# A decoder trunk's attention: how the first two groups load, keep and split their input blocks

## The chip, the core and the metric

The kernel runs on one core of one Trainium2 chip. A core has the engines TensorE (PE, matrix products), VectorE (DVE), ScalarE (ACT), GpSimd (POOL) and SyncE (SP, which here issues the DMA transfers), each with its own queue of instructions that it works through in order. The metric is the device time of one execution in microseconds (us), as the median of several.

## The reference

Two layers of a trunk over x of 1024 positions by 1024 channels, in float32. The first layer mixes by dilated sliding-window attention, the second by a gated recurrence, and after each comes a two-layer perceptron; every sub-layer ends in `x <- LayerNorm(alpha * x + sublayer(x))`. Cut to the part that the change is about:

```python
def dilated_attention_mixer(x, w_in, w_out):
    proj = (x @ w_in).reshape(B, S, N_GROUPS, 3, ATTN_HEADS, ATTN_HEAD_DIM)
    for g, (window, dilation) in enumerate(((128, 1), (512, 4), (2048, 16))):
        q, k = rotary(proj[:, :, g, 0], pos), rotary(proj[:, :, g, 1], pos)
        o, lse = dilated_window_attention(q, k, proj[:, :, g, 2], window, dilation)
    wts = softmax(stack(lses))
    return einsum('gbsh,gbshe->bshe', wts, stack(outs)) @ w_out
```

The second layer's recurrence also needs a few constants that depend on the weights alone (`forget_lower_bounds(lb_logits)`) and a causal mask.

## The kernel before

**Projections.** A unit is a pair of heads in one dilation. There are 24, taken two at a time: 12 groups. A group's q, k and v (j = 0, 1, 2: three pairs of weight blocks) are computed by the seven products of a Winograd-Strassen scheme, so a group is 21 products; product number n is 21 times the group, plus 3 times the place of the operand in `ORDA` = (2, 1, 6, 7, 4, 5, 3), plus j. The operand i is made of the transposed input's four blocks "11", "12", "21", "22" (`load_x`, two tiles of 128x1024 each): operands 1, 2 and 3 are the blocks "11", "21" and "22" themselves, 5, 6, 7 and 4 are the sums T1, T2, T3 and T4 (`combine_x`, on DVE). For float32 accuracy each operand, of x as of the weights, is split in a high half (a copy on ACT, line 131) and a low half (a subtraction on DVE, line 132), so a product is 12 matmuls of 128x512: xh by the weight's high half (line 644), xl by it (645), xh by the weight's low half (646).

**Where operands come from.** In group 0 `make_T` computes and splits each operand, and `keep_T` (line 371) spills the four tiles of its halves, 0.5 MB each, into the DRAM tensor xtd, one operand at each of the products in `KEEP`. In all later groups `get_T` (line 385) reads the halves back from xtd, the high half five products ahead and the low half three. Weights come by `load_w` (line 396, tiles wa and wb), are combined and split by `split_w_` (lines 409 to 417) and get their low half in `low_w` (line 425).

**What follows a product.** Its result (tile pmm in PSUM) is evicted by ACT (lines 667, 671) or added on DVE (669, 677, 679) into e, or vT for j = 2. A unit whose e are complete is rotated: `rope` moves e by four DMAs (line 453) into rot, POOL multiplies rot with the sine (455), DVE e with the cosine (456) and DVE adds the two (457) into qT or kT. Then come the scores s (line 483), the softmax (494, 497), the transposed probabilities (507, 510) and the output o (522). These steps of one group are placed between the products of the next, by the numbers in `ROPES` and `OFFS`. `constants` (line 432) loads cosine, sine, mask and the selector selw, which ACT copies to bsel (line 438), all at product 11. `hgrn_consts` (line 1353) computes the recurrent layer's constants by 29 small instructions on DVE and three on ACT, and loads its mask into cmf and casts it to cm; the program calls it after attention.

**Order.** A scheduler orders instructions on each engine by its own model, within the dependencies. The class `in_order` (line 101) adds dependencies so that an engine follows the order in which the program is written; in attention it holds for PE and DVE. ACT, POOL and SP are ordered by the scheduler, which also put most of `hgrn_consts` between the instructions of products 8 to 15. SP has eight semaphores for its transfers: from the ninth on an issue waits until the transfer eight places before has landed.

## Time and profile before

| | before |
|---|---|
| median of 3 runs | 2917.54 us (2911.75 to 2921.99) |
| the profiled execution | 2914.81 us, its span 2913.0 us |
| busy: PE, DVE, ACT, POOL | 2809.4, 2080.0, 1451.5, 430.4 us |
| mean granted TensorE clock | 0.986 of full speed |
| the DMA queue | 533.06 MB, 54.1% of the 16 engines' span |

The busy time of an engine is the sum of its instructions' durations; times in the rows below are counted from the start of the span. A start in brackets gives the idle time of the engine before that instruction and what ended it: `[2.26 <-DMA lg<-in_lb_logits_dram]` is 2.26 us of idleness that the landing of lg ended. The granted clock is the share of full speed that TensorE was given: 1.00 stands for 2.4 GHz, 0.50 for 1.2 GHz, and a stretch between them is a mixture.

### The profile page before, as it was taken

How to read it: one execution, taken by the hardware profiler on the slowest of the kernel's cores; microseconds unless marked ns; L12 is line 12 of the kernel's file. 1: busy time of each engine (PE TensorE's matmuls, PEld its weight loads, DVE VectorE, ACT ScalarE, POOL GpSimd, SP SyncE). 2: the span in 40 equal slices, each digit the busy share in tenths (PEclk: the TensorE clock that was granted, in tenths of full speed). 3: DMA queues.
4: the chain of work that ended last, by engine and by line, in shares of the span. 5: the costliest groups of instructions: out<-in, count | busy, mean ns of one | idle time of the engine just before them, and what ended most of it. 6: DMA issues, size and time to landing. Idle time of an engine off the chain costs nothing.

```text
span 2913.0 us, 40585 instructions
## 1 busy us (share of the span) xinstructions
PE 2809.4 (96%) x14152; PEld 2246.6 (77%) x14152; DVE 2080.0 (71%) x3717; ACT 1451.5 (50%) x3136; POOL 430.4 (15%) x211
## 2 busy tenths in 40 slices
PE   7899999999999999999999999999999999999998
PEld 6677777777777767788878886778787788878885
DVE  7678676777877668787677867555667787678776
ACT  5354555555455553644454535554553544454442
POOL 0112111111211102100061411101101200033300
PEclk9999999999999999999999999999999999999999
DMA  8876777678677533464484744101132465484653
GB/s 335 298 257 201 239 252 240 221 269 283 191 251 252 183 100 127 142 230 156 148 320 131 251 134 131 41 33 58 37 123 82 150 206 178 148 309 152 210 175 113
DMA packets 219325, 535.65 MB, mean 184 GB/s; under 512 B 32112, under 2 KB 46448, under 8 KB 219120
## 3 DMA queue, kind: packets, MB, share of 16 engines
q1 hardware_dynamic: 219120, 533.06, 54.1%
q8 instruction: 111, 1.82, 0.3%
q14 instruction: 94, 0.77, 0.1%
HBM read 408.96 MB, written 98.44 MB: 174 GB/s over the span
## 4 chain that ended last, share of the span: by engine, by line
PE 82%; DVE 7%; DMA 7%; issue 2%; ACT 1%; SPq 1%; POOL 0%; DVEq 0%; ACTq 0%; POOLq 0%
PE pup L1075 6%; PE pup L1073 6%; PE pup L1074 6%; PE pmm L645 6%; PE pmm L644 6%; PE pmm L646 6%; PE pdy L1214 4%; PE pdy L1213 4%; PE pdy L1210 4%; PE pmm L165 3%; PE pmm L166 3%; PE pmm L167 3%; PE pdx L1210 3%; PE pdx L1213 3%; PE pdx L1214 3%; PE s L483 2%
## 5 line engine op out<-in xcount | busy, mean ns | idle before, releaser
L644 PE MATMUL pmm<-xh,H 128*128 128x512 f32 x1008 | 411.0, 408 | 13.8 <-ACT H L417 8.0
L645 PE MATMUL pmm<-xl,H 128*128 128x512 f32 x1008 | 400.3, 397 | 14.3 <-DMA xl<-xtd 13.9
L646 PE MATMUL pmm<-xh,H 128*128 128x512 f32 x1008 | 399.4, 396 | 1.2 <-DVE H L425 1.2
L455 POOL TENSOR_TENSOR rot<-rot,sinT 128x1024 f32<-128x1024 f32 x48 | 141.7, 2956 | 858.9 <-DMA rot<-e 457.7
L644 PEld LDWEIGHTS pmm<-xh,H 128*128 128x128 f32 x1008 | 193.4, 192 | 54.8 <-ACT H L417 8.0
L645 PEld LDWEIGHTS pmm<-xl,H 128*128 128x128 f32 x1008 | 193.1, 192 | 54.5 <-DMA xl<-xtd 16.4
L646 PEld LDWEIGHTS pmm<-xh,H 128*128 128x128 f32 x1008 | 192.5, 191 | 43.8 <-DVE H L425 2.2
L494 DVE CUSTOM_DVE_ANT_0 p<-s,mask 128x128 f32<-128x128 f32 (+1 forms) x384 | 113.1, 348 | 139.8 <-PE s L483 129.8
L497 ACT ACTIVATE p<-p,stats 128x128 f32<-128x128 f32 (+1 forms) x384 | 168.2, 440 | 64.4 <-DVE stats L494 64.0
L1214 PE MATMUL pdy<-dT,dS 128*128 128x512 f32 x512 | 199.3, 389 | 0.0
L1213 PE MATMUL pdy<-dT,dS 128*128 128x512 f32 x512 | 199.3, 389 | 0.0
L1210 PE MATMUL pdy<-dT,dS 128*128 128x512 f32 x512 | 199.3, 389 | 0.0
L132 DVE TENSOR_TENSOR dS<-dr,dS 128x512 fp32r<-128x512 f32 x192 | 167.9, 874 | 22.8 <-ACT dS L131 22.4
L131 ACT ACTIVATE dS<-dr 128x512 fp32r<-128x512 f32 x192 | 119.9, 625 | 114.3 <-PE pdy L1214 57.5
L510 ACT ACTIVATE pts<-ppt 128x256 f32<-128x256 f32 (+1 forms) x192 | 85.6, 472 | 145.6 <-PE ppt L507 142.7
L165 PE MATMUL pmm<-f0nh,wh 128*128 128x512 f32 x384 | 153.3, 399 | 0.8 <-ACT wh L131 0.8
L167 PE MATMUL pmm<-f0nh,wl 128*128 128x512 f32 x384 | 150.0, 391 | 0.0
L166 PE MATMUL pmm<-f0nl,wh 128*128 128x512 f32 x384 | 149.9, 390 | 0.0
L1182 POOL TENSOR_TENSOR hold<-hold,dr 128x512 f32<-128x512 f32 x32 | 47.4, 1480 | 554.6 <-DVE upa L1115 517.5
L1034 ACT ACTIVATE H<-wc 128x512 fp32r<-128x512 f32 x128 | 77.2, 625 | 73.5 <-DVE wc L1027 44.2
L132 DVE TENSOR_TENSOR dT<-dr,dT 128x512 fp32r<-128x512 f32 x128 | 109.7, 862 | 4.2 <-ACT dT L131 3.5
L1213 PEld LDWEIGHTS pdy<-dT,dS 128*128 128x128 f32 x512 | 96.1, 188 | 20.1
(395 smaller groups left out, 7192.9 us busy)
## 6 DMA issues: line engine op xcount, KB each, us to landing
xh<-xtd SPq DMA_DIRECT2D x154, 512.0 KB
xl<-xtd SPq DMA_DIRECT2D x154, 512.0 KB
dr<-hd SPq DMA_DIRECT2D x192, 256.0 KB
dr<-in_w_down_dram SPq DMA_DIRECT2D x160, 256.0 KB
rot<-e SPq DMA_DIRECT2D x192, 128.0 KB
wa<-in_w_up_dram SPq DMA_DIRECT2D x48, 512.0 KB
wa<-in_w_attn_dram SPq DMA_DIRECT2D x36, 512.0 KB
wb<-in_w_attn_dram SPq DMA_DIRECT2D x36, 512.0 KB
```

The source lines that it names most:

```text
L132: nc.vector.tensor_sub(lo, raw, hi.bitcast(F32))
L165: nc.tensor.matmul(o, wh[:, k], xs.h(k), start=k == 0, stop=False)
L166: nc.tensor.matmul(o, wh[:, k], xs.l(k), start=False, stop=False)
L167: nc.tensor.matmul(o, wl[:, k], xs.h(k), start=False, stop=k == NK - 1)
L644: nc.tensor.matmul(o, wh, hi[k // 2][:, c], start=begin and k == 0, stop=False, skip_group_check=True)
L645: nc.tensor.matmul(o, wh, lo[k // 2][:, c], start=False, stop=False, skip_group_check=True)
L646: nc.tensor.matmul(o, wl, hi[k // 2][:, c], start=False, stop=end and k == 3, skip_group_check=True)
L1073: nc.tensor.matmul(o, wh, xf.h(b, k), start=begin and k == 0, stop=False, skip_group_check=True)
L1074: nc.tensor.matmul(o, wh, xf.l(b, k), start=False, stop=False, skip_group_check=True)
L1210: nc.tensor.matmul(o[q], h, T_[:, L], start=begin, stop=False, skip_group_check=True)
L1213: nc.tensor.matmul(o[q], h, T_[:, R], start=False, stop=False, skip_group_check=True)
L1214: nc.tensor.matmul(o[q], l, T_[:, L], start=False, stop=end, skip_group_check=True)
```

## The change

- 26 transposes of the identity, into a PSUM bank that nobody reads, stand ahead of all PE work.
- SP follows the written order up to the weights of the first eight products, in which the first weight now comes between the two halves of the first block of x; then SP and ACT follow it up to product 21.
- T1 and T2 are made one half after the other, and T2's split is postponed behind the work of products 2 and 3 (`soon`).
- The three operands that are plain blocks are not spilled in group 0. Group 1 reads the blocks of x again and splits them again, and spills them then. `KEEP` says at which product which operand is spilled.
- The selector's load, copy and a memset move from product 11 to product 36.
- `hgrn_consts` is called at product 40, inside the written order of DVE.

```diff
--- before.py
+++ after.py
@@ -47,7 +47,7 @@
 LOADW = 8
 SPLITW = 5
 UNIT0 = 3
-KEEP = (4,6,8,10,12,14,16)
+KEEP = {10: 2, 13: 3, 16: 4, 19: 5, 23: 7, 26: 8, 41: 13}
 MIX = (5, 6, 7, 10, 11, 12, 13, 14, 15)
 ROPES = ((-5, -2, -1, 2), (-4, 0, 1, 4))
 OFFS = ((0, 2, 4, 7, 9, 11), (10, 12, 15, 17, 19, 21))
@@ -313,7 +313,7 @@
         return t
 
 
-    def attention(pre):
+    def attention(pre, hc):
         cosT = U("cosT")
         sinT = U("sinT")
         units = [(pr, g) for pr in range(NPAIR) for g in GORD]
@@ -332,12 +332,17 @@
 
         xtd = dp.tile([7, 2, P, 2048], F32, name="xtd")
         opT, xr, xc = {}, {}, {}
-
-        def load_x(b):
+        soon = []
+
+
+        PLAIN = {1: "11", 2: "21", 3: "22"}
+
+        def load_x(b, between=lambda: None):
             half, k0 = int(b[1]) - 1, (int(b[0]) - 1) * 2048
             xr[b] = [U("x" + b) for _ in range(2)]
             for q in range(2):
                 nc.sync.dma_start(xr[b][q], xT[half, :, k0 + q * 1024:k0 + (q + 1) * 1024])
+                between()
 
         def combine_x(name, x, y, eng):
             xc[name] = [U("x" + name) for _ in range(2)]
@@ -347,13 +352,19 @@
         def make_T(i):
             v, g = nc.vector, nc.gpsimd
             if i == 6:
-                combine_x("T1", xr["12"], xr["11"], v)
-                combine_x("T2", xr["22"], xc["T1"], v)
+                for n_ in ("T1", "T2"):
+                    xc[n_] = [U("x" + n_) for _ in range(2)]
+                out_ = [U("xh", F32R) for _ in range(2)], [U("xl", F32R) for _ in range(2)]
+                for q in range(2):
+                    v.tensor_sub(xc["T1"][q], xr["12"][q], xr["11"][q])
+                    v.tensor_sub(xc["T2"][q], xr["22"][q], xc["T1"][q])
+                    soon.append(lambda q=q: split(xc["T2"][q], out_[0][q], out_[1][q]))
+                return out_
             elif i == 7:
                 combine_x("T3", xr["22"], xr["12"], v)
             elif i == 4:
                 combine_x("T4", xr["21"], xc["T2"], v)
-            src = {1: "11", 2: "21", 6: "T2", 7: "T3", 3: "22", 5: "T1", 4: "T4"}[i]
+            src = PLAIN.get(i) or {6: "T2", 7: "T3", 5: "T1", 4: "T4"}[i]
             src = xc.pop(src) if src == "T3" or src == "T4" else xc[src] if src in xc else xr[src]
             hi = [U("xh", F32R) for _ in range(2)]
             lo = [U("xl", F32R) for _ in range(2)]
@@ -368,7 +379,7 @@
         def keep_T(m):
             for n, part in enumerate(opT[m]):
                 for q in range(2):
-                    nc.sync.dma_start(xtd[ORDA[m] - 1, n][:, q * 1024:(q + 1) * 1024], part[q].bitcast(F32))
+                    nc.sync.dma_start(xtd[ORDA[m % 7] - 1, n][:, q * 1024:(q + 1) * 1024], part[q].bitcast(F32))
 
         def get_T(m, n):
             if m >= 7 * len(groups):
@@ -376,6 +387,12 @@
             i = ORDA[m % 7]
             if m < 7:
                 if m not in opT:
+                    opT[m] = make_T(i)
+                return
+            if m < 14 and i in PLAIN:
+                if n == 0:
+                    load_x(PLAIN[i])
+                else:
                     opT[m] = make_T(i)
                 return
             if m not in opT:
@@ -433,6 +450,8 @@
             nc.sync.dma_start(cosT, cos_t)
             nc.sync.dma_start(sinT, sin_t)
             nc.sync.dma_start(mask, masks)
+
+        def factor_constants():
             selw = wp.tile([P, 512], F32, name="selw", tag="p")[:, :NG * P]
             nc.sync.dma_start(selw, bsel)
             act(sel, selw, AF.Copy)
@@ -715,20 +734,29 @@
 
         order = in_order((mybir.EngineType.PE, mybir.EngineType.DVE))
         order.__enter__()
-        load_x("21")
-        for n in range(3):
+        for _ in range(26):
+            nc.tensor.transpose(bank("pt", "warm")[:, :P], ident, ident)
+        loads = in_order((mybir.EngineType.SP,))
+        loads.__enter__()
+        load_x("21", lambda: load_w(0))
+        for n in range(1, 3):
             load_w(n)
         get_T(0, 0)
         for b in ("11", "12", "22"):
             load_x(b)
         for n in range(LOADW):
             load_w(n)
+        loads.__exit__()
         for n in range(SPLITW):
             split_w_(n)
             if n <= SPLITW - 2:
                 low_w(n)
+        first = in_order((mybir.EngineType.SP, mybir.EngineType.Activation))
+        first.__enter__()
         for n in range(len(seq)):
             gi, i, j = seq[n]
+            if n == 21:
+                first.__exit__()
             load_w(n + LOADW)
             if j == 0:
                 get_T(n // 3 + 1, 1)
@@ -736,18 +764,24 @@
                 get_T(n // 3 + 2, 0)
             if n == 11:
                 constants()
+            if n == 36:
+                factor_constants()
+            if n == 40:
+                hc.extend(hgrn_consts())
             if n == len(seq) - 2 * PREA - 3:
                 early = pre(oN)
             if n >= len(seq) - 2 * PREA - 1:
                 next(early, None)
-            if n == 0:
-                get_T(2, 0)
             if n in KEEP:
-                keep_T(KEEP.index(n))
+                keep_T(KEEP[n])
             product(n)
             for f in fill.pop(n, []):
                 f()
+            if n == 0:
+                get_T(2, 0)
             low_w(n + SPLITW - 2)
+            if n > 1 and soon:
+                soon.pop(0)()
             split_w_(n + SPLITW)
             if n % 21 == 14:
                 last = gi == len(groups) - 1
@@ -1606,10 +1640,10 @@
     x3d = dp.tile([S, D], F32, name="x3d")
     x5d = dp.tile([S, D], F32, name="x5d")
     pr = Out(w_attn_out, "a", 0)
-    oN, fill = attention(pr.pre_steps)
+    hc = []
+    oN, fill = attention(pr.pre_steps, hc)
     xf, late = outproj_ln(pr, oN, fill, lambda t: x[t * P:(t + 1) * P, :],
                           ln_mix_g[0], ln_mix_b[0], x1d)
-    hc = hgrn_consts()
     gw = GateW()
     xs, late = ffn(0, xf, late, x1d, ln_ffn_g[0], ln_ffn_b[0], False, lambda: gw.prefetch(0))
     pr = Out(w_hgrn_out, "h", 1)
```

The first place is SP's queue at the start. Before (x_98 and x_99 are the two halves of block "21", wa the weights, xtd the spill tensor):

```order
1 L340 DMA x_98<-in_xT_dram 128x1024
2 L340 DMA x_99<-in_xT_dram 128x1024
3 L396 DMA wa<-in_w_attn_dram 128x1024 x3
4 L371 DMA xtd<-xh 128x1024 [waits Activation_49]
5 L340 DMA x_118<-in_xT_dram 128x1024
6 L340 DMA x_119<-in_xT_dram 128x1024
7 L340 DMA x_122<-in_xT_dram 128x1024 [waits DMAHW0_49]
8 L340 DMA x_123<-in_xT_dram 128x1024 [waits DMAHW1_49]
9 L340 DMA x_126<-in_xT_dram 128x1024 [waits DMAHW2_49]
10 L340 DMA x_127<-in_xT_dram 128x1024 [waits DMAHW3_49]
11 L396 DMA wb<-in_w_attn_dram 128x1024 [waits DMAHW4_49]
12 L396 DMA wb<-in_w_attn_dram 128x1024 [waits DMAHW5_49]
```

Now:

```order
1 L344 DMA x_150<-in_xT_dram 128x1024
2 L413 DMA wa<-in_w_attn_dram 128x1024
3 L344 DMA x_151<-in_xT_dram 128x1024
4 L413 DMA wa<-in_w_attn_dram 128x1024 x2
5 L1389 DMA lg<-in_lb_logits_dram 128x16
6 L1444 DMA hg<-in_hgrn_g_dram 128x8
7 L344 DMA x_170<-in_xT_dram 128x1024
8 L344 DMA x_171<-in_xT_dram 128x1024 [waits DMAHW0_49]
9 L344 DMA x_174<-in_xT_dram 128x1024 [waits DMAHW1_49]
10 L344 DMA x_175<-in_xT_dram 128x1024 [waits DMAHW2_49]
11 L344 DMA x_178<-in_xT_dram 128x1024 [waits DMAHW3_49]
12 L344 DMA x_179<-in_xT_dram 128x1024 [waits DMAHW4_49]
```

The first weight moved ahead of the second half of the first block; lg and hg, inputs of `hgrn_consts`, moved from behind the mask and the selector to the place in front of the other blocks of x; and the spill that stood there is gone.

The second place is SP's queue at the boundary of groups 0 and 1, around the first transfers of rot. Before:

```order
46 L371 DMA xtd<-xh 128x1024 [waits DMAHW7_49,Activation_49]
47 L385 DMA xh<-xtd 128x1024 [waits DMAHW0_49]
48 L385 DMA xh<-xtd 128x1024 [waits DMAHW1_49,PE_49]
49 L371 DMA xtd<-xh 128x1024 [waits DMAHW2_49,Activation_49]
50 L371 DMA xtd<-xl 128x1024 [waits DMAHW3_49,DVE_49]
51 L371 DMA xtd<-xl 128x1024 [waits DMAHW4_49,DVE_49]
52 L453 DMA rot<-e 32x1024 [waits DMAHW5_49,DVE_49]
53 L453 DMA rot<-e 32x1024 [waits DMAHW6_49]
54 L453 DMA rot<-e 32x1024 [waits DMAHW7_49]
```

Now (x_570 and x_571 are the halves of block "21", read a second time):

```order
30 L344 DMA x_570<-in_xT_dram 128x1024 [waits DMAHW6_49,DVE_49,Activation_49]
31 L344 DMA x_571<-in_xT_dram 128x1024 [waits DMAHW7_49,DVE_49]
32 L382 DMA xtd<-xh 128x1024 [waits DMAHW0_49]
33 L382 DMA xtd<-xh 128x1024 [waits DMAHW1_49]
34 L382 DMA xtd<-xl 128x1024 [waits DMAHW2_49]
35 L382 DMA xtd<-xl 128x1024 [waits DMAHW3_49]
36 L472 DMA rot<-e 32x1024 [waits DMAHW4_49,DVE_49,Activation_49]
37 L472 DMA rot<-e 32x1024 [waits DMAHW5_49]
38 L472 DMA rot<-e 32x1024 [waits DMAHW6_49]
```

The read of the first operand of group 1 moved: its halves were read back as xh in front of the rot transfers and as xl behind them; now its raw block stands in front of all of them, behind it one operand's spill.

The third place is product 40, on DVE, around the addition that evicts it (e<-pmm,e). Before:

```order
194 L494 ISA stats 128x1
195 L494 ISA p,stats<-s,mask 128x256
196 L494 ISA stats 128x1
197 L425 TENSOR_TENSOR H<-wa,H 128x512 [waits DMAHW6_49,Activation_49]
198 L679 TENSOR_TENSOR e<-pmm,e 128x512 [waits PE_49]
199 L457 TENSOR_TENSOR qT<-qT,rot 128x1024 [waits DMAHW1_49,DMAHW6_49,DMAHW0_49,DMAHW7_49,DVE_49,Pool_49]
200 L425 TENSOR_TENSOR H<-wa,H 128x512 [waits Activation_49]
201 L679 TENSOR_TENSOR vT<-pmm,vp 128x512 [waits PE_49]
202 L494 ISA p,stats<-s,mask 128x128 [waits PE_49]
```

Now (cmf is the mask's tile, hc the recurrent layer's constants):

```order
204 L1423 TENSOR_TENSOR hc_C<-hc_C,hc_Cm 128x8 [waits DVE_49]
205 L1424 TENSOR_SCALAR hc_Cm<-hc_Cm 128x8 [waits DVE_49]
206 L1425 TENSOR_TENSOR hc_C<-hc_C,hc_Cm 128x8 [waits DVE_49]
207 L1442 TENSOR_TENSOR hc_CA<-hc_C,hc_A 128x8 [waits DVE_49]
208 L1448 CAST cm<-cmf 128x512 [waits DMAHW0_49]
209 L698 TENSOR_TENSOR e<-pmm,e 128x512 [waits PE_49]
210 L476 TENSOR_TENSOR qT<-qT,rot 128x1024 [waits DMAHW6_49,DMAHW1_49,Pool_49]
211 L442 TENSOR_TENSOR H<-wa,H 128x512
212 L698 TENSOR_TENSOR vT<-pmm,vp 128x512 [waits PE_49]
```

The last of the 29 small instructions and the cast moved to the place in front of that addition. The same place on SP, where cmf is loaded, reads now:

```order
107 L402 DMA xl<-xtd 128x1024 [waits DMAHW3_49,PE_49]
108 L402 DMA xl<-xtd 128x1024 [waits DMAHW4_49,PE_49]
109 L413 DMA wb<-in_w_attn_dram 128x1024 [waits DMAHW5_49]
110 L402 DMA xh<-xtd 128x1024 [waits DMAHW6_49]
111 L402 DMA xh<-xtd 128x1024 [waits DMAHW7_49]
112 L1447 DMA cmf<-in_cmask_dram 128x512 [waits DMAHW0_49,PE_49]
113 L413 DMA wb<-in_w_attn_dram 128x1024 [waits DMAHW1_49]
```

Before, the load of cmf stood behind all of attention, and wb followed xh directly.

## Rows read from the trace of the kernel before

**Rows 1.** The page, part 4: the chain that ended last, by engine.

```profile
PE 82%; DVE 7%; DMA 7%; issue 2%; ACT 1%; SPq 1%; POOL 0%; DVEq 0%; ACTq 0%; POOLq 0%
```

**Rows 2.** PE's waits, 0 to 400 us: total us, times, longest us.

```profile
PE pmm L645 <- DMA xl<-xtd: 9.0, 3, 5.8
...
PE s L483 <- DVE kT L457: 0.8, 1, 0.8
```

**Rows 3.** PE, single matmuls of group 0: start, duration, idle before.

```profile
8.04 0.80 PE L644 MATMUL pmm<-xh,H 128*128 128x512 f32 x1 [8.04 <-ACT H L417]
...
14.42 0.39 PE L644 MATMUL pmm<-xh,H 128*128 128x512 f32 x1
...
22.67 0.50 PE L644 MATMUL pmm<-xh,H 128*128 128x512 f32 x1 [3.30 <-ACT e L667]
...
45.08 0.79 PE L646 MATMUL pmm<-xh,H 128*128 128x512 f32 x1 [1.24 <-DVE H L425]
...
48.23 0.42 PE L644 MATMUL pmm<-xh,H 128*128 128x512 f32 x1
...
48.95 0.40 PE L644 MATMUL pmm<-xh,H 128*128 128x512 f32 x1
```

**Rows 4.** Stretches: us, busy us of PE, PEld, DVE, ACT, POOL; PEclk, DMA, GB/s.

```profile
80.00:100.00 20.00, 12.41 (x44) 9.76 (x45) 15.70 (x11) 1.72 (x3) 7.58 (x3) 0.82 0.98 326
120.00:140.00 20.00, 20.00 (x111) 15.76 (x111) 5.09 (x20) 12.08 (x35) 0.00 (x0) 1.00 0.79 261
140.00:160.00 20.00, 20.00 (x122) 15.23 (x118) 11.97 (x32) 9.94 (x29) 0.22 (x1) 1.00 0.24 61
160.00:170.00 10.00, 10.00 (x62) 7.89 (x61) 9.47 (x19) 5.18 (x18) 4.83 (x2) 1.00 0.93 301
170.00:180.00 10.00, 9.63 (x54) 7.45 (x52) 9.97 (x8) 5.59 (x14) 2.92 (x1) 1.00 1.03 345
```

**Rows 5.** ACT, first loads, and the selector's copy.

```profile
5.99 1.06 ACT L131 ACTIVATE xh<-x 128x1024 fp32r<-128x1024 f32 x1 [0.23 <-DMA x<-in_xT_dram]
7.36 0.63 ACT L417 ACTIVATE H<-wa 128x512 fp32r<-128x512 f32 x1 [0.31 <-DMA wa<-in_w_attn_dram]
...
39.26 0.52 ACT L438 ACTIVATE bsel<-selw 128x384 fp32r<-128x384 f32 x1 [7.02 <-DMA selw<-in_bsel_dram]
```

**Rows 6.** DVE, the gaps before T3.

```profile
39.43 0.17 DVE L1364 TENSOR_TENSOR hc_mx<-lg 128x8 f32<-128x8 f32 x1 [2.26 <-DMA lg<-in_lb_logits_dram]
41.76 1.23 DVE L132 TENSOR_TENSOR xl<-xT,xh 128x1024 fp32r<-128x1024 f32 x1 [2.17 <-ACT xh L131]
```

**Rows 7.** SP, the first rot transfers.

```profile
69.38 10.88 SPq L453 DMA_DIRECT2D rot<-e  x8
```

**Rows 8.** DVE, boundary of groups 0 and 1.

```profile
84.27 4.08 DVE L457 TENSOR_TENSOR qT<-qT,rot 128x1024 f32<-128x1024 f32 x1 [7.20 <-DMA xl<-xtd]
...
96.48 2.79 DVE L425 TENSOR_TENSOR H<-wa,H 128x512 fp32r<-128x512 f32 x1
```

**Rows 9.** POOL at the same boundary.

```profile
95.79 2.93 POOL L455 TENSOR_TENSOR rot<-rot,sinT 128x1024 f32<-128x1024 f32 x1 [9.24 <-DMA rot<-e]
```

**Rows 10.** DVE, one pair of small constant instructions.

```profile
54.08 0.24 DVE L1373 TENSOR_TENSOR hc_e<-hc_e,hc_den 128x8 f32<-128x8 f32 x2
```

**Rows 11.** SP before product 40.

```profile
160.53 1.02 SPq L385 DMA_DIRECT2D xl<-xtd  x2
```

**Rows 12.** The tile cmf, its cast: durations in ns, first and last start in us.

```profile
L1414 DVE CAST cm<-cmf x1: 421/421/421, 1092.2 to 1092.2; 128x512 uint8<-128x512 f32 x1
```

**Rows 13.** DVE behind product 40.

```profile
163.04 0.69 DVE L679 TENSOR_TENSOR e<-pmm,e 128x512 f32<-128x512 f32 x1 [0.32 <-PE pmm L646]
...
178.94 1.21 DVE L457 TENSOR_TENSOR kT<-kT,rot 128x1024 f32<-128x1024 f32 x1
```

**Rows 14.** PE, scores of group 1's first unit, and product 46.

```profile
182.43 0.93 PE L483 MATMUL s<-kT,qT 64*128 64x128 f32 x8
...
184.14 0.48 PE L644 MATMUL pmm<-xh,H 128*128 128x512 f32 x1
```

## The prediction

> **What bounds the kernel now.** I read the page first: TensorE (PE) is busy nearly all of the span, and 82% of the chain that ended last is PE [rows 1]. A change pays only where PE stands still or runs at its lower clock. The list of PE's waits in the first 400 us comes next, since the change touches only the first two groups of attention [rows 2]: three waits for xl that is read back from DRAM, 9.0 us in all, and 0.8 for kT in front of the scores; a wait of 3.3 for an eviction on ScalarE (ACT) stands in the single rows of PE [rows 3]. The table of stretches shows what binds the engines there [rows 4]: from 80 to 100 us PE is busy 12.41 of 20 with the DMA engines at 0.98, from 160 to 170 VectorE (DVE) has 9.47 busy of 10. Between them (140 to 160) PE never waits and DVE has 8 us free. The single instructions follow, engine by engine, in the parts below. A measurement of this kernel tells about 0.3% (8.75 us) from no change.
>
> **Start of group 0.** Before, PE starts at 8.04, runs 15 matmuls in 6.38 us at the half clock (0.425 each), and from 14.42 on 21 more before the wait that ends at 22.67, which began 3.30 earlier, at 19.37: 0.236 each [rows 3]. Its first weight is split on ACT at 7.36 after the second piece of x at 5.99, so loads follow each other by 1.37 us [rows 5]. Now the first weight is loaded second and the second half of x third, and ACT in written order takes both halves of xh before it: xh at 7.36 for 1.06, then the weight for 0.63, so PE starts at about 9.05, 1.0 later. The DVE split of that half (1.23) and the low half of the weight (0.68) put the third matmul at 10.3. The 26 transposes are to bring the clock up before that; 34 matmuls at 0.236 then end at 18.3, 1.1 before 19.37. The eviction now stands ahead of T2's split on ACT, and the 3.3 us wait goes: a lead of 4.4 us.
>
> I don't let all of it stand. Products 6 to 9 need T2, T3 and the combined weights, all from DVE, which has one gap of 2.26 before 39.43 and another of 2.17 before 41.76 [rows 6]. The lead turns PE's early arrival into waits there. What falls away for DVE are these two gaps, 4.4 us, which hang on ACT's wait of 7.02 us for selw [rows 5]; the load of selw and its copy now come at product 36. The low half of product 9's weight let PE go on at 45.08 [rows 3]; it can come between 4.4 earlier and unchanged. I take 1.8 earlier: T1 and T2 are still made when the last piece of x has landed, and T2's second split moves behind other work, which eats the rest. From 45.08 to 48.23 PE then runs seven matmuls at 0.45; if the shorter waits leave the clock up, another 1.6 is won. **Term A: −3.4 us**, with −1.8 and −6 as ends.
>
> The Trainium skill, DMA: Bandwidth & Descriptors, Specifications, puts the smallest transfer at line rate at 512 B, and speaks against loading lg and hg (64 and 32 bytes in a partition) in front of six pieces of x; no row shows their price. Taken as 512 B in each of 128 partitions at the 0.5 MB in 1.37 us of these loads, an estimate, both together would delay x by 0.3 us, and the sum would be 0.3 higher.
>
> **The boundary to group 1.** Before, eight rot transfers take 10.88 us to issue, since SyncE (SP) waits for landings and spills stand in front of them [rows 7]; DVE is idle 7.20 us until 84.27 [rows 8], and PE waits for xl behind the same queue. The spills of three blocks (6 MB) leave group 0, and the raw blocks, half the bytes, are loaded ahead of the rots. So the transfers come early, and PE's 9.0 us for xl can go. What replaces it is DVE work: two blocks split again, four pieces of 1.23 us = 4.9 us, with four of ACT's about 1.06, in a stretch where DVE holds the scores back. They stand beside GpSimd's (POOL) rotary multiplications: a subtraction of 0.68 us took 2.79 at 96.48, next to the POOL instruction from 95.79 to 98.72 [rows 8, 9], so each meeting costs about 2.1. One such meeting and 4.9 us make 7.0 us against the 7.2 of idle time: kT is ready about when it was. Bounds: 9.8 us gained (all of the waits for xl and kT), 0 if kT binds. I take 0, less 0.4 of the lead that is lost on the way: the lead is **−3.0** after the boundary. The third block's split (2.5 us of DVE) and its spills fall at products 34 to 41; the splitting costs nothing, DVE's 8 free us of 140 to 160 hide it.
>
> **Product 40.** The constants of the recurrent layer, placed by the scheduler in DVE's gaps until now, stand in DVE's written order behind product 39's work and before the addition that evicts product 40. These are 29 small instructions; two in a row take 0.24 us where they are independent [rows 10], and about 0.2 each in a dependent row, and two trips to ACT lie between: 4.5 to 6 us, in a stretch with 0.5 us of free DVE. Behind them DVE waits for cmf, 0.26 MB, which SP issues behind two xl (from 160.53), wb and two xh [rows 11]: five times 0.52 MB and cmf, 2.9 MB, at the 301 GB/s of this stretch [rows 4] are 9.6 us after 160.53: it lands at 170.1. The cast (0.42 where it stands now [rows 12]) ends about 170.6, and the addition of 0.69 that began at 163.04 [rows 13] begins there: DVE is 7.6 us late. Who waits: product 43 (its low weight, its bank), then rot additions and kT, which ended at 178.94 + 1.21 = 180.15 while the scores began at 182.43 [rows 13, 14]. 2.3 us of slack, so PE loses 7.6 − 2.3 = 5.3; the POOL instruction that stretched DVE's work here may now pass beside the wait and give back 2.1. Bounds: 1 (the data lands while the small instructions run and only they count, less slack and the POOL meeting) and 7.6. **Term B: +5.6**, 0.3 above the difference for the dependent trips to ACT, and not near the lower end, as DVE is busy 9.97 of 10 us in the stretch that follows [rows 4]. The three spills that now precede kT's rot transfers (1.6 MB, 4.6 us at 345 GB/s [rows 4]) are covered by DVE's lateness; with DVE in time they would themselves make kT some 2 us late.
>
> **Nothing:** the load of cmf and its cast leave a later place where nobody waits. selw at product 36 is free in the uncrowded stretch. From product 49 on the order on all engines is that of before, and PE-bound groups pass a lead or a delay on in full.
>
> **Sum.** The profiled execution took 2914.81, its span 2913.0. −3.0 + 5.6 = +2.6, so 2917.4 for that execution; the median of the three runs lies 2.7 above it, so **2920** is forecast for the median, against 2917.54.
>
> **Rivals.** *The boundary pays* (faster). DVE's two splits fit in its idle time before the rots land, and kT comes early: 9.8 of waits less the 4.9 of DVE work gives 4.9, with A's 3.4 and the half-clock matmuls after 85.03 (0.2 us more each, some 12: 2.4), 10.7 in all, and product 40's term only 1 because cmf finds a queue that runs ahead: −9.7, **2908**. For it: six of 14 MB of spills go from a stretch at 0.98 DMA share. Against: the same 6 MB come back as spills in group 1, and DVE is at 15.7 of 20 there.
>
> *The wait for cmf decides* (slower). Place: DVE's cast before product 40's eviction; condition: cmf lands later than about 167, when the small instructions are through. If the spills moved into group 1 keep the queue full up to 160 (their 6 MB are 17 us of transfers; free DMA time from 120 to 160 is about 19), cmf lands some 3 us later, DVE is 11 late, PE loses 8.5, and a gap of that length is followed by matmuls at the half clock, as the rows from 45.08 to 48.23 show [rows 3]: 15 of them, 3 more. With A worth 1.8: +9.7, **2927**; with A at 0, 2929.
>
> *The change does not do what it says.* The transposes take too little to raise the clock before 9 us, or DVE binds products 6 to 9 just as before: A is 0, the rest as forecast, +5.6: **2923**.
>
> **How the numbers follow.** Forecast 0.52, boundary 0.23, cmf 0.18, no lead 0.07. Faster than 2908.8 needs the first rival and its better half or the lower tail of the forecast: 0.18. Slower than 2926.3 is most of the second rival and a little of the forecast: 0.20. The rest, 0.62, is no change. The range takes in the first rival, its better half down to 2904 (A at −6, B at 1), and the second up to 2930. The forecast's own range is 2913 to 2926.
>
> **What would show it.** Right: the first matmul near 9 us at the short pitch; no wait for ACT's e; product 10 at about 45.5 in place of 48.95 [rows 3]; the waits for xl at 85 and 98 gone, with the kT wait there; on DVE, a wait for cmf of some 3 us near 165 to 170 with the cast behind it, and PE waits of 5 to 6 us in all between 170 and 190. Wrong: DVE reaches the cast after cmf (product 46 then starts at 184.14 or before [rows 14]), or PE's waits between 80 and 110 us go with none in their place (the boundary paid), or a half-clock stretch behind product 43 or 45.

## The result and the profile after

The changed kernel took 2921.15 us (median of 20 runs, 2917.04 to 2929.96), the kernel before 2915.03 (median of 20, 2909.16 to 2923.62): a ratio of 1.0020, 95% interval 1.0011 to 1.0029, or 3 to 8 us more. The prediction was 2920, 2.6 us more than before. The profiled execution of the changed kernel took 2924.84 us, its span 2923.1.

On the page, PE's share of the chain is what it was; DVE's 7% has become 8%, and DMA's 7% is 5% [rows 1]:

```profile
PE 2821.8 (97%) x14178; PEld 2250.7 (77%) x14178; DVE 2103.5 (72%) x3724; ACT 1457.2 (50%) x3143; POOL 425.9 (15%) x211
...
PE 82%; DVE 8%; DMA 5%; issue 2%; ACT 1%; SPq 0%; POOL 0%; DVEq 0%; ACTq 0%; POOLq 0%
```

PE's waits from 0 to 400 us answer to [rows 2] (total, times, longest). The 9.0 us for xl are no longer in the list; waits for DVE stand in their place, for the low half of a weight (L665) and for kT. A wait of 2.7 is put down to ACT's xh; it belongs to product 21 and is read below. The wait for ACT's e moved from product 3 to product 9:

```profile
PE pmm L665 <- DVE H L442: 6.8, 7, 3.8
PE s L502 <- DVE kT L476: 4.1, 2, 3.0
...
PE pmm L663 <- ACT xh L131: 2.7, 1, 2.7
PE pmm L663 <- ACT e L690: 2.4, 1, 2.4
```

The stretches, with columns as in [rows 4] (busy us of PE, PEld, DVE, ACT, POOL; PEclk, DMA share, GB/s). From 10 to 16 us the granted clock is 0.50, right behind the warm-up; from 80 to 100 DVE is now at 19.97 of 20 (15.70 before). The third block's split went into DVE's free time at 140 to 160 (14.42 busy, 11.97 before) and cost PE nothing; behind product 40, from 170 to 180, PE is busy 7.58 of 10, at a clock of 0.83 (9.63 at 1.00 before):

```profile
10.00:16.00 6.00, 5.43 (x14) 4.14 (x14) 5.37 (x8) 4.32 (x7) 0.00 (x0) 0.50 1.02 398
80.00:100.00 20.00, 13.37 (x46) 9.37 (x44) 19.97 (x15) 2.83 (x5) 7.28 (x2) 0.80 1.04 344
140.00:160.00 20.00, 20.00 (x116) 15.33 (x115) 14.42 (x32) 12.67 (x32) 0.99 (x1) 1.00 0.46 130
160.00:170.00 10.00, 9.58 (x58) 7.18 (x56) 8.30 (x30) 5.12 (x17) 3.96 (x2) 1.00 0.94 325
170.00:180.00 10.00, 7.58 (x36) 5.45 (x37) 9.66 (x18) 3.88 (x14) 1.69 (x1) 0.83 1.04 363
```

PE, single instructions (start, duration, idle before). The warm-up ends at 7.94, the first matmul comes at 9.35, and the short matmuls of 0.39 us come back only with 16.81. 45.38 is the start of product 10 (48.95 before [rows 3]), 79.15 is product 21; 100.79 the first scores, which waited for kT; 171.42 product 43 and 173.15 its low half, both behind the late DVE; from 174.09 on the matmuls of product 43 last 0.63 and come 0.43 apart, where 0.39 and 0.23 are usual; 186.24 the scores that began at 182.43 before, and 187.94 product 46 (184.14 before [rows 14]):

```profile
1.42 6.52 PE L738 MATMUL warm<-ident 128*128 128x128 f32 x26 [1.42 <-POOL ident masks.py:199]
9.35 0.51 PE L663 MATMUL pmm<-xh,H 128*128 128x512 f32 x1 [1.41 <-ACT H L434]
...
10.69 0.79 PE L665 MATMUL pmm<-xh,H 128*128 128x512 f32 x1 [0.57 <-DVE H L442]
...
16.81 0.39 PE L664 MATMUL pmm<-xl,H 128*128 128x512 f32 x1
...
40.70 0.79 PE L663 MATMUL pmm<-xh,H 128*128 128x512 f32 x1 [2.44 <-ACT e L690]
...
45.38 0.39 PE L663 MATMUL pmm<-xh,H 128*128 128x512 f32 x1
...
79.15 0.47 PE L663 MATMUL pmm<-xh,H 128*128 128x512 f32 x1 [2.67 <-ACT xh L131]
...
100.79 1.23 PE L502 MATMUL s<-kT,qT 64*128 64x128 f32 x8 [3.05 <-DVE kT L476]
...
171.42 0.50 PE L663 MATMUL pmm<-xh,H 128*128 128x512 f32 x1 [1.84 <-DVE e L698]
...
173.15 0.50 PE L665 MATMUL pmm<-xh,H 128*128 128x512 f32 x1 [1.00 <-DVE H L442]
...
174.51 0.63 PE L663 MATMUL pmm<-xh,H 128*128 128x512 f32 x1
...
186.24 0.93 PE L502 MATMUL s<-kT,qT 64*128 64x128 f32 x8 [1.06 <-DVE kT L476]
...
187.94 0.48 PE L663 MATMUL pmm<-xh,H 128*128 128x512 f32 x1
```

DVE. The row at 73.79 is the second split of block "21", 86.14 that of "11"; 78.32 is the addition of product 18's result. 161.89 to 169.47 are the 29 small instructions, then come the cast with its wait and product 40's addition, which began at 163.04 before, and kT's at 184.97, before at 178.94 [rows 13]:

```profile
73.79 4.61 DVE L132 TENSOR_TENSOR xl<-x,xh 128x512 fp32r<-128x512 f32 x3
78.32 0.68 DVE L698 TENSOR_TENSOR e<-pmm,e 128x512 f32<-128x512 f32 x1
...
86.14 2.36 DVE L132 TENSOR_TENSOR xl<-x,xh 128x1024 fp32r<-128x1024 f32 x2
...
161.89 2.35 DVE L1398 TENSOR_TENSOR hc_mx<-lg 128x8 f32<-128x8 f32 x1
...
169.30 0.17 DVE L1442 TENSOR_TENSOR hc_CA<-hc_C,hc_A 128x8 f32<-128x8 f32 x1
170.34 0.43 DVE L1448 CAST cm<-cmf 128x512 uint8<-128x512 f32 x1 [0.87 <-DMA cmf<-in_cmask_dram]
170.68 0.68 DVE L698 TENSOR_TENSOR e<-pmm,e 128x512 f32<-128x512 f32 x1
...
184.97 1.22 DVE L476 TENSOR_TENSOR kT<-kT,rot 128x1024 f32<-128x1024 f32 x1
```

The view puts product 21's wait down to ACT's xh, which ended at 79.05. But that copy belongs to block "11", which product 21 does not read, and in f3 below product 21 starts at 80.34, before the same copy has ended (80.49). In all seven profiles that split "21" a second time product 21 starts 0.14 to 0.15 us behind the end of the addition that stands here at 78.32, and f3's row names it too. So PE waited for DVE, where this addition stood behind the second split:

```profile
80.34 0.47 PE L663 MATMUL pmm<-xh,H 128*128 128x512 f32 x1 [2.66 <-DVE e L698]
```

POOL beside the first of the small instructions:

```profile
161.68 2.54 POOL L474 TENSOR_TENSOR rot<-rot,sinT 128x1024 f32<-128x1024 f32 x1 [0.26 <-PE pmm L665]
```

So the two halves of the forecast can be followed on PE: 3.57 us ahead at product 10, 1.37 at product 27, 1.38 at product 42, 3.80 behind at product 46. The two profiled executions differ by 10.0 us at their ends, so 6.2 of it come later. In this pair of profiles the distance swings between 1.5 and 8.8 us in the rest of attention, at group boundaries with equal orders; single profiles differ so much there that only the medians of the whole kernel decide.

### The profile page after: what moved, and what is told of

It reads as the page before. It is cut to its first block, busy times and chain, and to the rows that moved or that the text cites. A ratio compares the mean times of both kernels' runs of the same rounds, so it can differ in the third digit from the quotient of the medians.

```text
span 2923.1 us, 40634 instructions
## 1 busy us (share of the span) xinstructions
PE 2821.8 (97%) x14178; PEld 2250.7 (77%) x14178; DVE 2103.5 (72%) x3724; ACT 1457.2 (50%) x3143; POOL 425.9 (15%) x211
## 3 DMA queue, kind: packets, MB, share of 16 engines
q8 instruction: 112, 1.84, 0.3%
## 4 chain that ended last, share of the span: by engine, by line
PE 82%; DVE 8%; DMA 5%; issue 2%; ACT 1%; SPq 0%; POOL 0%; DVEq 0%; ACTq 0%; POOLq 0%
PE pup L1109 7%; PE pup L1107 7%; PE pup L1108 6%; PE pmm L663 6%; PE pmm L664 6%; PE pmm L665 6%; PE pdy L1247 4%; PE pdy L1244 4%; PE pdy L1248 4%; PE pmm L165 3%; PE pmm L166 3%; PE pmm L167 3%; PE pdx L1247 3%; PE pdx L1248 3%; PE pdx L1244 3%; PE s L502 2%
## 5 line engine op out<-in xcount | busy, mean ns | idle before, releaser
L665 PE MATMUL pmm<-xh,H 128*128 128x512 f32 x1008 | 401.9, 399 | 6.8 <-DVE H L442 6.8
L665 PEld LDWEIGHTS pmm<-xh,H 128*128 128x128 f32 x1008 | 193.2, 192 | 52.7 <-DVE H L442 10.7
L1244 PEld LDWEIGHTS pdy<-dT,dS 128*128 128x128 f32 x512 | 96.1, 188 | 20.1
L1248 PEld LDWEIGHTS pdy<-dT,dS 128*128 128x128 f32 x512 | 96.1, 188 | 20.0
```

What stands on the lines that cost most here:

```text
L665: nc.tensor.matmul(o, wl, hi[k // 2][:, c], start=False, stop=end and k == 3, skip_group_check=True)
L1244: nc.tensor.matmul(o[q], h, T_[:, L], start=begin, stop=False, skip_group_check=True)
L1248: nc.tensor.matmul(o[q], l, T_[:, L], start=False, stop=end, skip_group_check=True)
```

## The experiments

Starts of products are read from PE's single instructions of each profile; a table gives them against the kernel before (22.67, 48.95, 112.52, 167.95 and 184.14 us for products 3, 10, 27, 42 and 46). Ratios are to the kernel before on the same chip, with their 95% interval.

Each kernel has one profile, and two cautions follow. The change, e1, e2, e3, f1 and f5 are written alike up to product 30, yet their profiles differ by 3.15 us at product 3, 1.84 at product 10 and 2.03 at product 27, so a smaller difference there shows nothing. And a profiled execution need not be a typical one: e1's was its fastest (2910.91 us), f3's and g2's the slowest of their twelve (2923.63 and 2915.14).

### Product 40: which of the costs?

| kernel | product 3 | 10 | 27 | 42 | 46 | median us, ratio to before |
|---|---|---|---|---|---|---|
| change | -1.33 | -3.57 | -1.37 | -1.38 | +3.80 | 2921.15, 1.0020 [1.0011, 1.0029] |
| e1 | -1.51 | -4.51 | -2.15 | -2.15 | +1.92 | 2919.96, 1.0014 [1.0003, 1.0024] |
| e2 | -2.82 | -2.67 | -0.35 | -0.36 | +3.50 | 2916.70, 1.0006 [0.9997, 1.0015] |
| e3 | -1.47 | -3.71 | -1.54 | -1.54 | +3.24 | 2919.21, 1.0014 [1.0005, 1.0023] |
| e5 | +0.16 | -0.47 | -0.74 | -0.74 | +7.71 | 2922.17, 1.0025 [1.0014, 1.0036] |
| f1 | -1.12 | -3.51 | -1.19 | -1.21 | -1.38 | 2914.13, 0.9989 [0.9980, 0.9998] |
| f5 | -4.27 | -3.28 | -0.12 | -0.13 | +4.61 | 2921.42, 1.0012 [1.0001, 1.0022] |

**e1: all constants at product 31.**

```diff
-            if n == 40:
+            if n == 31:
                 hc.extend(hgrn_consts())
```

> The changed kernel with hgrn_consts (29 small instructions, load and cast of cmf) called at product 31 in place of product 40. Theory (the constants at product 40 cost PE about 5 us there): product 43 starts near 169.4 and product 46 near 182.8 (1.4 before the kernel before, as at product 42), DVE does the constants at 122 to 130 in its free time, and the median is about 5 us under that of the change, so 1 below to 1 above the kernel before. Rival (the loss comes from the second split of blocks and from later boundaries, and what happens at product 40 is absorbed by product 70): product 46 at 182.8 as well, but the median stays 4 to 7 above the kernel before.

Half of it came. DVE did the constants at 123 to 129 us without a wait for cmf, and products 43 to 45 kept the lead (product 43 started 2.15 ahead). But product 46 was 1.92 behind, and the median only 0.6 thousandths under the change's ratio, with intervals that overlap. PE's rows show a wait that the first loss had covered: xl of the operand of product 45, queued behind the spill of block "22" that the change put at product 41.

```profile
179.25 0.50 PE L664 MATMUL pmm<-xl,H 128*128 128x512 f32 x1 [3.13 <-DMA xl<-xtd]
...
186.06 0.48 PE L663 MATMUL pmm<-xh,H 128*128 128x512 f32 x1
```

**e2: only the cast and load of cmf moved back**, behind attention. The 29 instructions stay.

```diff
+    def hgrn_mask():
+        cm = cp.tile([P, 512], U8, name="cm")
+        cmf = wp.tile([P, 512], F32, name="cmf", tag="p")
+        nc.sync.dma_start(cmf, cmask)
+        nc.vector.tensor_copy(cm, cmf)
...
+    hc.append(hgrn_mask())
     gw = GateW()
```

> The changed kernel with only the load and the cast of cmf behind attention, where they were; the 29 small instructions stay at product 40. Theory (small instructions and the landing of cmf lie over each other, each as long as the other): the addition of product 40 ends about 1.3 earlier than in the change (170.7 to 169.4), product 46 starts at 186.5 to 187.5, 3 or more behind the kernel before. Rival of the prediction (the wait for cmf decides): product 46 back at 183 to 184.

As expected on PE: 3.50 behind at product 46. The small instructions alone held product 40's addition to 170.27, from 162.79 on, 7.5 us:

```profile
162.79 2.35 DVE L1398 TENSOR_TENSOR hc_mx<-lg 128x8 f32<-128x8 f32 x1
...
170.27 0.68 DVE L698 TENSOR_TENSOR e<-pmm,e 128x512 f32<-128x512 f32 x1
```

**e3: the 29 instructions at product 31, cast and load of cmf at 40.**

```diff
+            if n == 31:
+                hc.extend(hgrn_consts())
             if n == 40:
-                hc.extend(hgrn_consts())
+                hc.append(hgrn_mask())
```

> The changed kernel with the 29 small instructions at product 31, the load and the cast of cmf still at product 40. Theory (two costs that lie over each other): the wait for cmf, 0.87 us in the change, now shows in full, 6 to 7 us on DVE from about 162.7 until the data lands at 169 to 170; the addition of product 40 begins at 170 to 170.7 and product 46 at 187 to 188, as in the change. Rival (the small instructions alone make the loss): the wait is under 2 us and product 46 starts at 183 to 184.

The wait shows in full, 8.50 us where 6 to 7 were expected, and the addition came at 170.11, product 46 at 187.38. Either cause alone holds the addition until 170.1 or later. The spill at product 41 stands in e2 and e3 too, but it acts later, at product 45, as e1 shows. From product 42 to 44, ahead of that, PE loses 4.97 us in the change, 3.72 in e2 and 4.56 in e3: either cause alone makes most of this loss.

```profile
169.77 0.43 DVE L1453 CAST cm<-cmf 128x512 uint8<-128x512 f32 x1 [8.50 <-DMA cmf<-in_cmask_dram]
```

**f5: the spill of "22" at product 46, constants at 40; f1: both moved.**

```diff
-KEEP = {10: 2, 13: 3, 16: 4, 19: 5, 23: 7, 26: 8, 41: 13}
+KEEP = {10: 2, 13: 3, 16: 4, 19: 5, 23: 7, 26: 8, 46: 13}
```

> The changed kernel with the spill of the third plain block at product 46 in place of 41, the constants still at product 40. Theory (the costs lie over each other): product 44 loses 4 to 5 us as in the change, product 46 starts at 186 to 188 and gains at most 1.5 against the change's 187.9. Rival (the spill makes the loss): product 46 at 184 or earlier.

> The changed kernel with hgrn_consts at product 31 and the spill of the third plain block at product 46 in place of 41. With the constants alone at 31, products 43 to 45 kept their lead of 2.15 over the kernel before and product 46 lost 4.06, on a wait of 3.1 for xl that stood behind that spill on the DMA queue. Theory (the spill is a second cost, hidden under the first): no wait for xl at product 45, product 46 starts 1.5 to 2.2 before the kernel before (182.0 to 182.6). Rival (the queue is full there without the spill too): product 46 still 1 or more behind the kernel before.

With the constants at 40 the spill's place changed nothing (product 46 was 4.61 behind; it started at 188.75, 0.75 later than expected). With both moved, the wait for xl shrank to 0.44 and product 46 came 1.38 ahead, narrowly under the 1.5 expected:

```profile
177.50 0.50 PE L664 MATMUL pmm<-xl,H 128*128 128x512 f32 x1 [0.44 <-DMA xl<-xtd]
...
182.76 0.48 PE L663 MATMUL pmm<-xh,H 128*128 128x512 f32 x1
```

From product 42 to 46 the four kernels lost 5.18 (change), 4.07 (e1), 4.74 (f5) and −0.17 (f1). The costs don't add, they lie over each other: constants or spill, each alone, cost 4 to 5 us, and only without both is the loss gone. The whole kernel's ratios, 1.0020, 1.0014, 1.0012 and 0.9989, set f1 apart in the same way; it alone of the four is under the kernel before. They do not follow product 46 closely, though: e2 and f3 are 3.50 and 4.57 behind there, and their ratios, 1.0006 and 1.0002, are not clear of 1.

**e5: the kernel before with hgrn_consts at product 40 alone.**

```diff
+            if n == 40:
+                hc.extend(hgrn_consts())
...
-    hc = hgrn_consts()
```

> The kernel before with one part of the change alone: hgrn_consts called at product 40 in DVE's written order. Theory: product 46 starts 4.5 to 6.5 later than in the kernel before (188.6 to 190.6), and the median rises by 4 to 6 us. Rival (the loss needs the spills that the change moved into group 1, and their fuller queue): product 46 under 3 us later, the median within 2 us.

The median rose by 6.8 us and product 46 came 7.71 late, more than in the change and than expected. cmf is issued at the same place of SP's queue, at 162.96, but DVE waited 4.26 for it until 174.14, 11.2 us after the issue, where it was 7.9 in the change (162.43 to 170.34). From issue to landing the DMA engines moved 310 GB/s at a share of 0.97, where the change has 367 at 0.99, so data flowed more slowly there; why it did, with fewer spills in the queue, is open. PE waited 5.00 for the addition. SP's, DVE's and PE's rows:

```profile
162.96 1.36 SPq L1415 DMA_DIRECT2D cmf<-in_cmask_dram  x1
```

```profile
174.14 0.43 DVE L1416 CAST cm<-cmf 128x512 uint8<-128x512 f32 x1 [4.26 <-DMA cmf<-in_cmask_dram]
```

```profile
175.22 0.79 PE L644 MATMUL pmm<-xh,H 128*128 128x512 f32 x1 [5.00 <-DVE e L679]
```

### Start and group 0

| kernel | product 3 | 10 | 27 | 42 | 46 | median us, ratio to before |
|---|---|---|---|---|---|---|
| change | -1.33 | -3.57 | -1.37 | -1.38 | +3.80 | 2921.15, 1.0020 [1.0011, 1.0029] |
| f3 | -3.17 | -2.78 | -1.00 | -1.02 | +4.57 | 2916.39, 1.0002 [0.9993, 1.0010] |
| g2 | +0.15 | -4.69 | -3.74 | -3.75 | -0.82 | 2910.08, 0.9979 [0.9967, 0.9991] |

**f3: the change without the 26 transposes.**

```diff
-        for _ in range(26):
-            nc.tensor.transpose(bank("pt", "warm")[:, :P], ident, ident)
```

> The changed kernel without the 26 transposes. Theory (DVE sets the end of products 6 to 9): PE starts at about 9.3 at the half clock, products 0 to 2 end some 2.5 us later, product 3 at 23 to 24.5 (change 21.3), but product 10 starts within 0.7 of the change's 45.4 and product 27 too; the median is that of the change. Rival (the warm-up makes the lead): product 10 2.5 us later, and product 27 as late as in the kernel before or later.

Both were wrong about product 3: it came 1.84 us earlier than in the change, though f5, with the warm-up, was earlier still (18.40). Without the warm-up the first seven matmuls take 0.58 to 0.79 us each and the short ones begin at 12.88, while the view gives a granted clock of 1.00 from 8 us on. Product 10 came 0.79 later than in the change, just over the theory's bound of 0.7, and product 27 0.37, both within the spread of profiles. Product 9 shows best that the first 20 us are gone by then: it starts between 40.35 and 40.70 in all eleven versions of the changed kernel, whose product 3 lies anywhere from 18.40 to 21.55, and DVE is busy for 9.96 of the 10 us from 30 to 40, here as in the change. Inside product 9 the two part again: from 44 to 46 us the granted clock was 0.50 here and 0.98 in the change.

The median is 4.8 us under the change's, and the ratios, 1.0002 and 1.0020, have intervals that don't meet. Why is open: the profile shows no gain (product 46 is 0.77 behind the change), and g1 against f2 below shows none either. That the warm-up costs the whole of the change's kernel some us is not ruled out.

```profile
9.25 0.79 PE L663 MATMUL pmm<-xh,H 128*128 128x512 f32 x1 [9.25 <-ACT H L434]
...
12.88 0.40 PE L664 MATMUL pmm<-xl,H 128*128 128x512 f32 x1
...
19.50 0.39 PE L663 MATMUL pmm<-xh,H 128*128 128x512 f32 x1
...
46.17 0.63 PE L663 MATMUL pmm<-xh,H 128*128 128x512 f32 x1
```

**g2: the kernel before with the selector's load and copy (and the memset beside them) at product 36 alone.**

```diff
+        def factor_constants():
...
             if n == 11:
                 constants()
+            if n == 36:
+                factor_constants()
```

> The kernel before with the selector's load and copy alone moved from product 11 to 36. Theory (term A: ACT's wait of 7.0 us for selw held back the split of T3): no wait of ACT near 32 to 39, product 9's xh 1 to 2.5 us earlier and product 10 at 46.5 to 48 in place of 48.95. Rival (T3 waits for DVE, or for lg on DVE, anyway): product 10 within 0.5 of 48.95.

ACT's copies of T3 started at 36.94 in place of 40.69, DVE's wait for lg fell from 2.26 to 0.53, and PE went from product 8 to 9 with 0.33 of idle time and without a slow stretch: product 10 at 44.26, 4.69 earlier, about twice the most that was expected; the change and its five likes have 2.67 to 4.51 there. The median is 6 us under the kernel before (0.9967 to 0.9991): as far as the intervals tell, this one move is worth as much as any version here. The profile doesn't show where. Only 0.82 of the lead is left at product 46, since product 45 waited 2.03 for xl (until 176.55), with neither the constants nor the moved spill in this kernel.

```profile
36.94 1.06 ACT L131 ACTIVATE xh<-xT 128x1024 fp32r<-128x1024 f32 x1
```

```profile
38.58 0.17 DVE L1368 TENSOR_TENSOR hc_mx<-lg 128x8 f32<-128x8 f32 x1 [0.53 <-DMA lg<-in_lb_logits_dram]
```

```profile
41.87 0.50 PE L648 MATMUL pmm<-xh,H 128*128 128x512 f32 x1 [0.33 <-DVE H L425]
...
44.26 0.39 PE L646 MATMUL pmm<-xh,H 128*128 128x512 f32 x1
```

### The boundary of groups 0 and 1

| kernel | product 3 | 10 | 27 | 42 | 46 | median us, ratio to before |
|---|---|---|---|---|---|---|
| f1 | -1.12 | -3.51 | -1.19 | -1.21 | -1.38 | 2914.13, 0.9989 [0.9980, 0.9998] |
| f2 | -1.74 | -3.25 | -6.12 | -6.14 | -5.29 | 2909.37, 0.9976 [0.9965, 0.9987] |
| g1 | -2.34 | -3.00 | -4.94 | -4.95 | -5.40 | 2910.82, 0.9976 [0.9965, 0.9987] |
| g3 | -4.13 | -2.57 | -5.62 | -5.64 | -6.57 | 2910.51, 0.9979 [0.9968, 0.9989] |
| g4 | -3.06 | -2.47 | -1.94 | -1.95 | -1.92 | 2911.88, 0.9982 [0.9971, 0.9994] |

**f2: f1, with "21" and "11" spilled in group 0 and read back in halves.**

```diff
-KEEP = {10: 2, 13: 3, 16: 4, 19: 5, 23: 7, 26: 8, 46: 13}
+KEEP = {4: 0, 7: 1, 10: 2, 13: 3, 16: 4, 19: 5, 46: 13}
...
-            if m < 14 and i in PLAIN:
+            if m < 14 and i == 3:
```

> The kernel f1 with two of the three plain blocks (21 and 11) spilled in group 0 after all, at products 4 and 7, where the DMA engines of the change are at 0.42 share, and read back in halves; only 22 is read again as a raw block. Theory (the second splits, 4.9 us of DVE at 0.98 busy, take the lead at the boundary): products 21 to 24 keep it, product 21 starts near 75.3 (before 78.9, change 79.2) and product 27 at 108 to 110 (before 112.5, change 111.2), the median some 2 us under f1. Rival (rot and the halves queue behind each other again as in the kernel before): waits for xl of several us at products 21 to 24 and product 27 at 111 or later.

(The diff is against the change; the constants' line is that of e1.) Product 27 came at 106.40, better than expected, 4.93 before f1. That four splits of 1.23 us are 4.92 is no proof that this is their price: f2 also moves the spills, and it is free of f1's waits of 3.81 for DVE's H and 3.06 for kT. Product 21, at 77.02, kept less than expected. A wait for xl did come back, at product 24, but it cost less than what went:

```profile
93.53 0.79 PE L664 MATMUL pmm<-xl,H 128*128 128x512 f32 x1 [6.71 <-DMA xl<-xtd]
```

The median (of six runs) is 4.8 us under f1 and 0.9965 to 0.9987 of the kernel before: with g1, g2 and g3, the fastest measured.

**g1 and g3: f2 without transposes, and with 34.**

```diff
-        for _ in range(26):
+        for _ in range(34):
             nc.tensor.transpose(bank("pt", "warm")[:, :P], ident, ident)
```

(g1 leaves both lines out.)

> The kernel f2 without the 26 transposes. In the change without them product 3 came 1.8 earlier, since the granted clock fell to 0.50 after the warm-up and stayed there until 16 us. Theory (the start is free of consequence, DVE binds until product 9): product 3 earlier by 1 to 2, product 10 within 0.7 of f2, the median within 2 of f2. Rival (the warm-up costs the whole kernel, as the medians of the change with and without it suggest, 2921 and 2916): the median 4 to 5 under f2.

> The kernel f2 with 34 transposes in place of 26, so that PE is busy until its first operands are there (26 ended at 7.9, the first matmul came at 9.35). Theory (the pause behind the warm-up lets the clock fall): no stretch at 0.50 before 20 us, product 3 at 19 or earlier (f2 20.9), product 10 within 0.7 of f2. Rival (the sparse first matmuls let it fall, or it falls at random): a stretch at 0.50 between 10 and 16 us again.

Product 3 moved by 2.4 us between f2 and g3, product 10 by 0.7 at most, and all three medians lie within 1.5 us. In g3's profile, with 34 transposes, the granted clock stays at 1.00 from 8 to 16 us, where f2 had 0.74 (8 to 10) and 0.52 (10 to 16):

```profile
8.00:10.00 2.00, 2.00 (x10) 1.25 (x9) 1.18 (x2) 1.83 (x3) 0.00 (x0) 1.00 1.06 387
10.00:16.00 6.00, 5.40 (x24) 4.41 (x24) 5.36 (x8) 4.69 (x7) 0.00 (x0) 1.00 1.03 404
```

**g4: f2 with the last spill of group 0 at product 26.**

```diff
-KEEP = {4: 0, 7: 1, 10: 2, 13: 3, 16: 4, 19: 5, 46: 13}
+KEEP = {4: 0, 7: 1, 10: 2, 13: 3, 16: 4, 26: 5, 46: 13}
```

> The kernel f2 with the last spill of group 0 at product 26 in place of 19. In f2 product 24 waited 6.7 us for an xl that was issued behind that spill (2 MB, 5 us of transfers). Theory (the queue order at the boundary sets product 24): that wait falls to 1 to 3 us and product 27 starts 2 to 4 us earlier than in f2 (106.4), the median 2 to 4 lower. Rival (kT's rotation binds next): the wait for xl gives way to one for kT in front of the scores, product 27 within 1 of f2.

A miss. The wait at product 24 fell to 1.85, but one of 6.02 for xl appeared at product 21, with 2.14 for kT behind it, and product 27 came 4.2 later than in f2. The time moved to another wait; the medians don't tell the two kernels apart (ratios 0.9982 and 0.9976). What SP's queue held in front of that xl was not tried further.

```profile
83.16 0.79 PE L664 MATMUL pmm<-xl,H 128*128 128x512 f32 x1 [6.02 <-DMA xl<-xtd]
...
95.79 0.50 PE L664 MATMUL pmm<-xl,H 128*128 128x512 f32 x1 [1.85 <-DMA xl<-xtd]
...
100.76 0.71 PE L502 MATMUL s<-kT,qT 64*128 64x128 f32 x8 [2.14 <-DVE kT L476]
```

## Why the prediction was right, and where it was not

The time, its sign and the class (no change by 0.3%) came as forecast, and so did the two terms: a lead in group 0 and a loss at product 40. That 2920 lies so near 2921.15 is in part luck: it was counted from a median of three runs, 2917.54, 2.5 us above that of twenty, and this hid that the 2.6 forecast are less than half of the 6.1 measured. Step by step:

**Start.** PE was forecast at 9.05 and 10.3, measured at 9.35 and 10.69: the load order was read rightly. The step "The 26 transposes are to bring the clock up before that" failed: the clock was granted during the warm-up and fell behind it, and product 3 came at 21.34, a lead of 1.33 in place of 4.4. The count behind it ("34 matmuls at 0.236 then end at 18.3") was right where the clock stayed: product 3 came at 18.40 in f5 and 18.54 in g3. The first 15 matmuls of the kernel before were called "at the half clock"; that is their pitch, and the view gives a granted clock of 1.00 there.

**Term A** was still right, since DVE binds products 6 to 9: product 10 was forecast at about 45.5, measured at 45.38 (3.57 earlier; −3.4 taken). f3, g1 and g3 show it: 2 us at product 3 are under 0.8 at product 10. The closeness is luck, since the five kernels that are written like the change had 2.67 to 4.51 there. The cause named, ACT's wait for selw, is shown by g2 in the kernel before, where it alone gave 4.69 against the 1.8 plus 1.6 taken. Whether the rest of the change took some of that back is not shown: the load order, T1 and T2 by halves and the postponed split were not run alone.

**The boundary** was the step furthest off on the gain side: a lead of 3.0 was to be left, 1.37 was. The price was right: 4.9 us and one meeting with POOL, 7.0 in all, were forecast, and the second splits took 4.61 + 2.36 = 6.97. What failed is "against the 7.2 of idle time": the idle 7.20 us of DVE were not there to pay it, since rot came earlier and its work moved up, and DVE was busy 19.97 of 20 us. PE waited for DVE at product 21 already, and then for H and kT.

**Term B** had nearly the right size (+5.6; from product 42 to 46 it was 5.18) and the right lateness of DVE against the kernel before: 7.6 us forecast, 170.68 − 163.04 = 7.64 measured. That the two agree is partly luck. The 7.6 were counted from the times of the kernel before and the lead was then added, as if cmf landed earlier by the lead; it did not, so against PE's lead of 1.38 DVE was 9.0 late. It made 1.6 of this good before kT, which stands 184.97 − 178.94 = 6.03 behind. PE's waits from 170 to 190 were 3.9 us in all (1.84, 1.00 and 1.06), where 5 to 6 were named, and about 1.6 came from eight long matmuls behind product 43 (granted clock 0.83 from 170 to 180): the half-clock stretch that the prediction had listed as a sign of being wrong, and that its sum left out.

The split was wrong. A wait of some 3 us for cmf was forecast and was 0.87; the small instructions took 7.58, not 4.5 to 6, since the first, forecast at 0.2 like the others, took 2.35 beside POOL's rotation, and most of the others depend on the one ahead, at 0.2 each, with waits of 0.28 and 0.21 for ACT between. It made no difference to the sum: cmf landed at 170.3 (170.1 forecast) and held the addition to that time anyway, as e3 shows. The second rival, "the wait for cmf decides", is thereby neither alone right nor refuted: it decides as soon as the small instructions are gone.

**The spill of "22"** was rightly said to be covered by DVE's lateness and to cost something without it, but at "some 2 us" by kT; alone it cost 4.07, mostly by xl behind it on the queue.

**The sum** of +2.6 compares with 3.80 at product 46 and 6.1 in the medians, whose interval begins at 3. At product 46 the boundary's 1.6, less the 0.4 that B was taken too high, make the difference of 1.2. Behind it, "PE-bound groups pass a lead or a delay on in full" held within the groups and failed at their boundaries: in these two profiles 3.80 became 1.5 and later 8.8. How much of the 6.1 arises there is not settled.

## What to carry to other kernels

Before an edit is undone or blamed, ask which other cost ends at the same time: of constants, mask and spill, taking any one away gave back little on PE, and only taking away all of them gave back all. Work without urgency (constants, selectors, casts, spills) belongs in the stretch where its engine has proven free time, and a load for it ahead of the saturated part of the queue; moving one small copy out of a full queue was worth, by the medians, as much as the best version that has all the other edits, though its profile does not show where. Rereading raw data saves transfers but pays in the engine that splits it, so it helps only where that engine, not the queue, has slack: here the third block's split cost PE nothing, and that of "21" held up product 21.

## What the runs showed of the hardware

- A busy PE at the start did not keep its clock. In the change 26 transposes ran for 6.5 us, PE then stood still for 1.41, and the granted clock was 0.50 (1.2 GHz) from 10 to 16 us. In one profile with 34 transposes, up to 9.4, it stayed at 1.00; without any, the matmuls were short from 12.88 on. In six other profiles with 26 it was 0.50 to 0.75 there, but in f5, with a pause of 1.61, 1.00, so the pause alone does not settle it.
- At the start the granted clock of the view did not tell the pitch. In the kernel before the first matmuls came about 0.43 us apart until 14.42 [rows 3], in f3 they were long until 12.88, and the view gives 1.00 from 8 us on in both.
- A DVE instruction on 128x8 (the maximum of two tiles) took 2.35 us from 161.89, beside POOL's multiplication from 161.68 to 164.22; the same instruction took 0.16 in e1, with POOL idle. The Trainium skill, SBUF — State Buffer, Terms, says that these two engines share a pair of ports and that the one that does not get them is blocked for the whole of the other's instruction; by that rule the small instruction ends just after 164.22, and the trace, with 164.24, agrees.
